# S5's feedthrough table by products on four column tiles, two masked copies and four shifted DMAs, with the first table loads on GpSimd's queue

## Chip, cores and metric

The kernel runs on one core of one Trainium2 chip. The metric is the device time of one execution in microseconds (us), lower is better. The engines are TensorE (PE, with its weight loads as PEld), VectorE (DVE), ScalarE (ACT), GpSimd (POOL) and SyncE (SP), which mostly issues DMAs.

## The reference

A decoder trunk of two layers on x (256 rows of 1024, float32). Each layer is: half a SwiGLU feed-forward block, a token mixer, half a SwiGLU feed-forward block, each behind an RMS norm and added to h. Layer 0 mixes with S5, a diagonal state-space layer; layer 1 with block-sparse attention.

```python
def s5_mixer(h, w_in, a_re, a_im, log_dt, b_re, b_im, c_re, c_im, d_skip, w_glu, w_out):
    u = h @ w_in
    lam = exp((a_re + i a_im) * exp(log_dt))        # 64 groups of 64 states
    # per group of 16 channels: state[t] = lam * state[t-1] + B u[t];  y[t] = Re(C state[t])
    y = y + d_skip * u
    g = gelu(y)
    g = g * sigmoid(g @ w_glu)
    return g @ w_out
```

So y is, for each group of 16 channels, a causal convolution of u with the taps C lam^k B, and d_skip added to the tap at distance 0.

## The kernel before

The trunk runs phase by phase: f00 (feed-forward), s5, f01, f10, moba, f11. Weights stream from HBM through three raw buffers on SP's DMA queue; ACT and DVE split each into a high and a low part in fp32r (L84 and L85, or with a gain L90 and L91), and PE makes three products for one (L397 to L399, L424, L425, L428). `st.pump()` starts such splits; SP's next weight load waits until a raw buffer has been split.

S5 handles four time steps at a time. For each block b of 128 channels (eight of them, as four groups of 32 channels, the index q) it reads three tables from DRAM scratch: dA (from input to state), dE (phases), and dB, of which columns 0 to 1023 lead from state to output and columns 1024 to 1535 are the feedthrough table: per q a matrix of 128 x 128, input step s and channel by output step t and channel, zero where t is before s, else the tap at distance t - s, with d_skip on the tap at distance 0. Within 32 channels there are two groups of 16 that must not mix, so products over 32 channels are masked by group.

The tables depend on weights alone. The generator `tables` makes them while f00 runs: its pieces are put, by a clock in units of matmul work (`slot`), between f00's matmuls, so the order on each engine is fixed in the program. An early part on POOL computes the sines and powers of lam (L691 to L697, behind POOL's part of the first norm, L1363 and following), DVE then makes the phases E (L631) and, block by block, the products `ZC`. `spread(b)` copies them into `TT` and `MPs[b]` with the groups apart (L857, L858) and writes `TT` to dB (L860); `d_diag(b)` puts d_skip on a diagonal. Then `t3_tab(b)` makes the feedthrough table (L878 to L895): eight f32 matmuls of 32 output rows and 64 columns into the first 32 partitions of a PSUM tile, one for each q and each of the real and the imaginary part (L887); one more that adds the diagonal (L889); eight ACT copies with a scale `gm` of 0 or 1 by group (L893), which place the taps for input step s at partitions 32s and at output steps s to 3 of the tile `t3`, whose other places were zeroed once (L647); and one DMA to dB (L895). `t1_tab` transposes and writes dA (L867 to L870).

When all is made, the tables' memory is given up, a pool for the loads takes its place, and the first three blocks' loads TA, TE and TB are issued on SP's queue (L944 to L962). SP takes its instructions in order, so S5's fourth w_in load and the loads of w_glu stand behind them. In S5, `w_in` multiplies (L982 scales by the norm, from POOL's L346 to L308), `t1` uses TA on PE (L991), `rot` uses TE on DVE and POOL (L1011 to L1023), and `y_out` uses TB (L1048 to L1050). The later loads follow on SP as buffers come free.

Near the start, DVE's queue holds the copy of transposed parameters `prm` (L671), the mask gm (L674) and `are` (L631) ahead of the splits of x (`xa`, L1346) that PE waits for; POOL makes `i16` (L676).

Of the kernel before, what the change touches and what calls it, by code (L numbers as in the profile page):

```python
# [10 lines left out]
F32 = mybir.dt.float32  # L11
F32R = mybir.dt.float32r
AF = mybir.ActivationFunctionType
OP = mybir.AluOpType
AX = mybir.AxisListType
# [103 lines left out]
def trunk_kernel(ctx: ExitStack, tc, x, ffn_norm, ffn_w_gate, ffn_w_up, ffn_w_down, mix_norm,  # L119
# [3 lines left out]
    nc = tc.nc  # L123
# [13 lines left out]
    def psR():  # L137
        return pp.tile([128, 512], F32, name="pR", tag="R", bufs=2)
# [4 lines left out]
    mm = nc.tensor.matmul  # L143
# [4 lines left out]
    dA = [dp.tile([128, 1024], F32, name=f"dA_{b}") for b in range(NB)]  # L148
    dE = [dp.tile([128, 4 * EW], F32, name=f"dE_{b}") for b in range(2)]
    dB = [dp.tile([128, 1536], F32, name=f"dB_{b}") for b in range(NB)]  # L150
# [84 lines left out]
    ident = cst[:, 0:128]  # L235
# [30 lines left out]
    if "s5" in phases:  # L266
        rho = cp.tile([128, 32], F32, name="rho")
        tstack, lstack, xstack = ExitStack(), ExitStack(), ExitStack()
        tabp = tstack.enter_context(tc.tile_pool(name="tab", bufs=1))
        scn = tabp.tile([32, 2, 128], F32, name="scn")  # L270
        ldt = tabp.tile([32, 2], F32, name="ldt")
        dnat = tabp.tile([32, 32], F32, name="dnat")
        nc.gpsimd.dma_start(ldt, s5_log_dt[0].rearrange("(q g) -> q g", g=2))
        nc.gpsimd.dma_start(scn[:, 0, :], s5_a_re[0].rearrange("(q g) p -> q (g p)", g=2))
        nc.gpsimd.dma_start(scn[:, 1, :], s5_a_im[0].rearrange("(q g) p -> q (g p)", g=2))
        nc.gpsimd.dma_start(dnat, s5_d[0].rearrange("(q c) -> q c", c=32))
    st = Stream(nc, units, rp, hp)

    gT = cp.tile([128, 48], F32, name="gT")
# [343 lines left out]
    def tables(tp):  # L623

        V, P = nc.vector, nc.gpsimd

        def T(name, *shape):
            return tp.tile([128] + list(shape), F32, name=name)
# [9 lines left out]

        MPs = [T(f"mp{k}", 2, 4, 4, 2, 16) for k in range(2)]
        TT = T("tt", 2, 4, 4, 2, 16)  # L640
        t3s = [T(f"t3{k}", 4, 4, 32) for k in range(2)]
        cf7 = T("cf7", 7, 2)
        for k, n in enumerate(range(15, 1, -2)):
            for i in range(2):
# [21 lines left out]
        ps = psR()  # L666
# [2 lines left out]
        nc.tensor.transpose(ps[:, 64:96], dtb.rearrange("q g p -> q (g p)"), ident[0:32, 0:32])  # L669
        prm = T("prm", 3, 32)  # L670
        V.tensor_copy(prm.rearrange("p a b -> p (a b)"), ps[:, 0:96])  # L671
        gm = tp.tile([32, 2], F32, name="gm")
        i2 = ident[0:32, 0:32].rearrange("p (g n) -> p g n", g=2)
        V.reduce_sum(gm, i2, axis=AX.X)  # L674
        i16 = tp.tile([32, 16], F32, name="i16")
        P.tensor_tensor(i16, i2[:, 0], i2[:, 1], op=OP.add)  # L676
        dTq = T("dTq", 32)
        ar, ai, dt = prm[:, 0, :], prm[:, 1, :], prm[:, 2, :]
        are, aim, mag = T("are", 32), T("aim", 32), T("mag", 32)
        tt(are, ar, dt, OP.mult)  # L680
# [3 lines left out]
        yield  # L684

        ps = psR()
        nc.tensor.transpose(ps[0:32, 0:32], dnat, ident[0:32, 0:32])
        V.tensor_copy(dTq[0:32, :], ps[0:32, 0:32])

        def pt(o, a, b, op):  # L690
            P.tensor_tensor(o, a, b, op=op)  # L691
# [33 lines left out]
        q, y, y2, e0, e1, den = (T(n, 32) for n in ("q", "y", "y2", "e0", "e1", "den"))  # L725
# [125 lines left out]
        def spread(b):  # L851

            d_diag(b)
            tv, mv = (o.rearrange("p i q s g n -> p (i q) s g n") for o in (TT, MPs[b % 2]))
            zv = ZC[b].rearrange("p m i q (s n) -> p m (i q) s n", n=16)
            for g, r in enumerate(HALF):
                nc.scalar.activation(tv[r, :, :, g, :], zv[r, 0, :, 1:5], AF.Copy)  # L857
                nc.scalar.activation(mv[r, :, :, g, :], zv[r, 1, :, 1:5], AF.Copy)  # L858
            for i in range(2):
                nc.gpsimd.dma_start(dB[b][:, 512 * i:512 * i + 512].rearrange("p (q x) -> p q x", q=4),  # L860
                                    TT[:, i].rearrange("p q t g n -> p q (t g n)"))
# [10 lines left out]
        DG = {}  # L872

        def d_diag(b):
            DG[b] = tp.tile([32, 4, 16], F32, name="dg", bufs=2)
            P.tensor_tensor(DG[b], i16[:, None, :].to_broadcast([32, 4, 16]),
                            dTq[0:32, 4 * b:4 * b + 4, None].to_broadcast([32, 4, 16]), op=OP.mult)

        def t3_tab(b):

            t3 = t3s[b % 2]
            ps = psR()
            zc = ZC.pop(b)
            pk = ps[0:32, 0:256].rearrange("p (q t c) -> p q t c", q=4, c=16)
            for qq in range(4):
                for i in range(2):
                    mm(ps[0:32, qq * 64:(qq + 1) * 64], MPs[b % 2][:, i, qq, 3].rearrange("p g n -> p (g n)"),  # L887
                       zc[:, 0, i, qq, 0:64], start=qq == 0 and i == 0, stop=False, skip_group_check=True)
            mm(pk[:, :, 0, :], ident[0:32, 0:32], DG.pop(b), start=False, stop=True, skip_group_check=True)  # L889
            tv = t3.rearrange("p q t (g c) -> p q t g c", c=16)  # L890
            for s in range(4):
                for g in range(2):
                    nc.scalar.activation(tv[32 * s:32 * s + 32, :, s:4, g, :], pk[:, :, 0:4 - s, :], AF.Identity,  # L893
                                         scale=gm[:, g:g + 1])
            nc.gpsimd.dma_start(dB[b][:, 1024:1536], t3.rearrange("p q t c -> p (q t c)"))  # L895

        work = []

# [10 lines left out]
        def add_spread(b):  # L909
            work.append((0.0, B_AT, (spread, b), [(t3_tab, b), (t1_tab, b, 0), (t1_tab, b, 1)], 3 * (b - 1)))  # L910
# [15 lines left out]
        while work or later or dma:  # L926
# [4 lines left out]
            if later and later[0][0] <= now:  # L931
                f = later.pop(0)
                f[1](*f[2:])
                done[0] += 1
            while work and work[0][1] <= now and credit >= work[0][0] and done[0] >= work[0][4]:
                w, _, f, pe, _ = work.pop(0)
                f[0](*f[1:])
                credit -= w
                t = max([now + LAG] + [a[0] + PACE for a in later])
# [2 lines left out]
        tstack.close()  # L942
        LP.append(lstack.enter_context(tc.tile_pool(name="load", bufs=3)))
        for b in range(3):  # L944
            ld_a(b)
            ld_e(b)
        for b in range(3):
            ld_b(b)

    LP, TA, TE, TB = [], {}, {}, {}  # L950

    def ld_a(b):
        TA[b] = LP[0].tile([128, 1024], F32, name="TA", bufs=3)
        nc.sync.dma_start(TA[b], dA[b])

    def ld_e(b):
        TE[b] = LP[0].tile([128, 2, 4, 65], F32, name="TE", bufs=3)
        nc.sync.dma_start(TE[b], dE[b // 4].rearrange("p (i q c) -> p i q c", i=2, c=65)[:, :, (b % 4) * 4:(b % 4) * 4 + 4])

    def ld_b(b):  # L960
        TB[b] = LP[0].tile([128, 1536], F32, name="TB", bufs=3)
        nc.sync.dma_start(TB[b], dB[b])  # L962


    def s5(nxt, entry):
# [60 lines left out]
        def t1ld(b):  # L1026
            t1(b)
            if b + 3 < NB:
                ld_a(b + 3)
# [5 lines left out]
        def rot_ld(b):  # L1035
            rot(b)
            if 0 < b < NB - 2:
                ld_e(b + 2)
# [269 lines left out]

    pre = []
    tab = tables(tabp) if "s5" in phases else iter(())  # L1310
    next(tab, None)
    slot = [0]
# [72 lines left out]
    ps = psR()  # L1385
# [73 lines left out]
```

## Time and profile before

| | |
|---|---|
| median of 3 runs | 992.19 us (992.04 to 992.23) |
| the profiled execution: its time, its span | 992.93 us, 991.2 us |
| granted TensorE clock | 1.000 |
| PE, PEld, DVE, ACT, POOL busy | 980.8, 878.8, 702.9, 575.9, 167.4 us |
| L893, ACT's copies of the feedthrough table | x64, 287 to 468 ns each, 97.0 to 200.4 us |
| DMAs of the feedthrough table (L895) | x8, 256 KB each, median 3.6 us from issue to landing |
| loads TA, TE, TB | x8 each, 512, 260 and 768 KB, median 5.5, 4.6 and 6.3 us to landing |

Times in a row are microseconds from the span's start; the span is from the first to the last instruction of the profiled execution, and a little time lies around it. A row of the timeline gives start, length, engine, line, operation, output<-input by the program's names, shapes and a count; the bracket at its end gives the engine's idle time before it and what ended that. Matmul rows overlap: a row's length is that of one matmul from its first to its last part, and the step from start to start is what it costs. An f32 matmul stands as two records. In a row of `L887 ... 106/110/110`, the three numbers are least, median and greatest length in ns.

### The profile page before, as it was taken

Reading aid. Unit: us, or ns where it says so; the run is one execution under the profiler, and the core shown is the slowest. Engines: PE = TensorE matmul, PEld = TensorE weight load, DVE = VectorE, ACT = ScalarE, POOL = GpSimd, SP = SyncE. Lnnn points to the kernel's source line nnn. Section 1 sums busy time; section 2 is a strip of 40 time slices with the busy share of each in tenths; the row PEclk is TensorE's granted clock in tenths of the full one; section 3 lists DMA queues with packets and bytes.
Section 4 is the critical chain, followed back from the end, with each engine's and each line's share of the span. In section 5 each row is a group of like instructions: output and inputs, shape, how many; then the busy total and the mean of one; then the engine's idle time right before and its main releaser. Section 6 shows DMA issues by size and latency. Waiting matters only on the chain.

```text
span 991.2 us, 16683 instructions
## 1 busy us (share of the span) xinstructions
PE 980.8 (99%) x6448; PEld 878.8 (89%) x6448; DVE 702.9 (71%) x1147; ACT 575.9 (58%) x1045; POOL 167.4 (17%) x330
## 2 busy tenths in 40 slices
PE   9999999999999999999999999999999999999998
PEld 7778888888998999999989999999888899999997
DVE  5699676857978677666657776665689667776663
ACT  6647778754246655555545555553798665655551
POOL 5881222103750100000010000000442010000000
PEclk9999999999999999999999999999999999999999
DMA  8978776887735566555626765655344456666531
GB/s 236 277 262 256 264 256 213 268 300 261 268 126 197 191 209 213 179 205 183 200 86 216 237 226 172 212 171 175 129 165 135 166 169 215 210 217 207 176 129 42
DMA packets 138080, 198.64 MB, mean 200 GB/s; under 512 B 16321, under 2 KB 109585, under 8 KB 137745
## 3 DMA queue, kind: packets, MB, share of 16 engines
q1 hardware_dynamic: 133808, 184.32, 57.0%
q0 software_dynamic: 3616, 12.66, 3.3%
q8 instruction: 50, 0.82, 0.3%
q10 hardware_dynamic: 576, 0.61, 0.3%
q14 instruction: 30, 0.24, 0.1%
HBM read 183.89 MB, written 13.66 MB: 199 GB/s over the span
## 4 chain that ended last, share of the span: by engine, by line
PE 89%; DVE 5%; POOL 3%; issue 1%; ACT 1%; DMA 1%; SPq 0%; ACTq 0%; DVEq 0%
PE pM L557 12%; PE pM L556 12%; PE pM L558 12%; PE pA L428 9%; PE pA L424 9%; PE pA L425 9%; PE pM L397 5%; PE pM L398 5%; PE pM L399 5%; DVE wlo L85 1%; POOL sc L691 1%; PE pR L331 1%; PE pR L887 1%; PE pR L867 1%; DVE zo L1016 1%
## 5 line engine op out<-in xcount | busy, mean ns | idle before, releaser
L556 PE MATMUL pM<-xa,whi 128*128 128x256 f32 x1056 | 293.0, 277 | 0.0
L557 PE MATMUL pM<-xa,whi 128*128 128x256 f32 x1056 | 292.3, 277 | 0.0
L558 PE MATMUL pM<-xa,wlo 128*128 128x256 f32 x1056 | 291.8, 276 | 0.0
L91 DVE SCALAR_TENSOR_TENSOR wlo<-raw,gT,whi 128x512 fp32r<-128x512 f32 x328 | 228.1, 748 | 69.6 <-ACT whi L90 69.3
L85 DVE TENSOR_TENSOR wlo<-raw,whi 128x1024 fp32r<-128x1024 f32 (+1 forms) x157 | 191.7, 1235 | 57.0 <-ACT whi L84 53.1
L90 ACT ACTIVATE whi<-raw,gT 128x512 fp32r<-128x512 f32 x328 | 213.6, 711 | 17.7 <-PE pA L428 13.6
L557 PEld LDWEIGHTS pM<-xa,whi 128*128 128x128 f32 x1056 | 198.5, 188 | 0.3
L556 PEld LDWEIGHTS pM<-xa,whi 128*128 128x128 f32 x1056 | 198.3, 188 | 0.0
L558 PEld LDWEIGHTS pM<-xa,wlo 128*128 128x128 f32 x1056 | 198.3, 188 | 0.0
L84 ACT ACTIVATE whi<-raw 128x1024 fp32r<-128x1024 f32 (+1 forms) x157 | 160.9, 1049 | 27.1 <-DMA raw<-in_ffn_w_down_dram 7.4
L424 PE MATMUL pA<-whi,ah 128*128 128x512 f32 x352 | 138.5, 394 | 0.0
L428 PE MATMUL pA<-whi,al 128*128 128x512 f32 (+1 forms) x409 | 137.8, 360 | 0.0
L425 PE MATMUL pA<-wlo,ah 128*128 128x512 f32 x352 | 137.4, 390 | 0.0
L571 ACT ACTIVATE sg<-gr 128x256 f32<-128x256 f32 x66 | 27.6, 418 | 158.7 <-DVE gr L568 158.7
L397 PE MATMUL pM<-whi,xa 128*128 128x512 f32 x288 | 119.4, 415 | 0.0
L398 PE MATMUL pM<-wlo,xa 128*128 128x512 f32 x288 | 112.9, 392 | 0.2 <-DVE wlo L91 0.2
L399 PE MATMUL pM<-whi,xa 128*128 128x512 f32 x288 | 113.0, 392 | 0.0
L428 PEld LDWEIGHTS pA<-whi,al 128*128 128x128 f32 x409 | 76.8, 188 | 16.4
L346 POOL TENSOR_TENSOR ms<-ss 128x1 f32<-128x1 f32 x10 | 1.9, 194 | 466.8 <-ACT sq L343 466.8
L424 PEld LDWEIGHTS pA<-whi,ah 128*128 128x128 f32 x352 | 66.1, 188 | 11.5
L425 PEld LDWEIGHTS pA<-wlo,ah 128*128 128x128 f32 x352 | 66.1, 188 | 11.3
L568 DVE TENSOR_TENSOR gr<-pM,rrow 128x512 f32<-128x512 f32 x66 | 45.5, 689 | 33.9 <-PE pM L558 33.8
(266 smaller groups left out, 1274.0 us busy)
## 6 DMA issues: line engine op xcount, KB each, us to landing
raw<-in_ffn_w_down_dram SPq DMA_DIRECT2D x44, 1024.0 KB, 5.3
raw<-in_ffn_w_gate_dram SPq DMA_DIRECT2D x80, 512.0 KB, 4.0
raw<-in_ffn_w_up_dram SPq DMA_DIRECT2D x80, 512.0 KB, 5.2
raw<-in_moba_w_qkv_dram SPq DMA_DIRECT2D x12, 1024.0 KB, 5.1
TB<-dB SPq DMA_DIRECT2D x8, 768.0 KB, 6.3
raw<-in_ffn_w_gate_dram SPq DMA_DIRECT2D x16, 256.0 KB, 4.3
raw<-in_ffn_w_up_dram SPq DMA_DIRECT2D x16, 256.0 KB, 4.6
dB<-tt POOLq DMA_DIRECT2D x16, 256.0 KB, 4.4
```

Source lines behind the costliest of these rows:

```text
L85: nc.vector.tensor_tensor(lo[:, c], r[:, c], hi[:, c].bitcast(F32), op=OP.subtract)
L90: nc.scalar.activation(hi[:, c], r[:, c], AF.Identity, scale=g)
L91: nc.vector.scalar_tensor_tensor(lo[:, c], r[:, c], g, hi[:, c].bitcast(F32), op0=OP.mult, op1=OP.subtract)
L397: mm(o, xh, wh, start=start, stop=False)
L398: mm(o, xh, wl, start=False, stop=False)
L399: mm(o, xl, wh, start=False, stop=stop)
L424: mm(o, xh, wh[:, c], start=first and kk == kks[0], stop=False)
L425: mm(o, xh, wl[:, c], start=False, stop=False)
L428: mm(o[:, a:a + w], xl, wh[:, n * 512 + a:n * 512 + a + w], start=False, stop=stop)
L556: mm(o, a, xh, start=k == 0 and i == 0, stop=False, skip_group_check=True)
L557: mm(o, a, xl, start=False, stop=False, skip_group_check=True)
L558: mm(o, b, xh, start=False, stop=k == 7, skip_group_check=True)
```

## The change

The feedthrough table is made in another form. `t3_tab(b)` now writes the four q onto four column tiles of PE (32 output rows each, PSUM partitions 32q to 32q + 31), 64 columns each: 4 products of the real part, 4 of the imaginary part, and 4 that add the diagonal, each with 32 columns of the 128 x 128 identity against `DG`, now 128 x 16. Two ACT copies of all 128 partitions, masked by group, put the four taps into `t3`, now 7 steps x 2 groups x 16 with the first three steps zero. The placing by input step is left to four DMAs of 64 KB each: for s, all partitions read 128 elements that begin at step 3 - s, and go to rows 32s to 32s + 31 of dB.

So d_skip is loaded as 8 x 128 in place of 32 x 32 and transposed to `dT` of 128 x 8; the masks `gm` and `i16` are made for 128 partitions, both by reductions on DVE; `d_diag` is one product with a scalar per partition.

The first loads of TA, TE and TB, three blocks, go to POOL's queue in place of SP's.

On PE, at the first table, there stands before (`zc` are the products, `mp` the spread copies, `dg` the diagonal, `whi`, `wlo` and `xa` f00's operands):

```order
L397 MATMUL pM<-whi,xa 128x512
L398 MATMUL pM<-wlo,xa 128x512
L399 MATMUL pM<-whi,xa 128x512
L887 MATMUL pR<-zc,mp_143 32x64 x8
L889 MATMUL pR<-dg,cst 32x4x16
L397 MATMUL pM<-whi,xa 128x512
L398 MATMUL pM<-wlo,xa 128x512
```

And now:

```order
L397 MATMUL pM<-whi,xa 128x512
L398 MATMUL pM<-wlo,xa 128x512
L399 MATMUL pM<-whi,xa 128x512
L885 MATMUL pR<-zc,mp_143 32x64 x8
L888 MATMUL pR<-dg,cst 32x16 x4
L397 MATMUL pM<-whi,xa 128x512
L398 MATMUL pM<-wlo,xa 128x512
```

The place among f00's matmuls is the same; the one diagonal matmul has become four, and the eight alternate between column tiles.

On DVE, at the start of the program, where PE waits for `xa`, there stands in the difference:

```order
 L85 TENSOR_TENSOR wlo<-raw,whi 128x1024
 L671 COPY prm<-pR 128x96
-L674 TENSOR_REDUCE gm<-cst 32x2
+L673 TENSOR_REDUCE gm<-cst 128x2
+L674 TENSOR_REDUCE i_245<-cst 128x16
 L631 TENSOR_TENSOR are<-prm 128x32
 L1346 SCALAR_TENSOR_TENSOR xa<-pA_253,gT,xa 128x256
```

One reduction has grown and a second has come ahead of `are` and `xa`; on POOL, L676 has gone, so that L1363 follows the memsets.

On POOL, at the end of the table work and ahead of the norm of S5's input, there stands before:

```order
L723 DMA dE_89<-e 128x2080
L870 DMA dA_87<-t_2188 128x512
L870 DMA dA_87<-t_2218 128x512
L346 TENSOR_TENSOR ms<-ss 128x1
L347 TENSOR_SCALAR ms<-ms 128x1
```

And now:

```order
L867 DMA dA_87<-t_2218 128x512
L954 DMA TA<-dA_80 128x1024
L958 DMA TE<-dE_88 128x2x260
L954 DMA TA<-dA_81 128x1024
L958 DMA TE<-dE_88 128x2x260
L954 DMA TA<-dA_82 128x1024
L958 DMA TE<-dE_88 128x2x260
L962 DMA TB<-dB_90 128x1536
L962 DMA TB<-dB_91 128x1536
L962 DMA TB<-dB_92 128x1536
L346 TENSOR_TENSOR ms<-ss 128x1
```

The nine loads have come between the last table's DMA and the norm; on SP they are gone from between the third and the fourth w_in load.

```diff
-        dnat = tabp.tile([32, 32], F32, name="dnat")
+        dnat = tabp.tile([8, 128], F32, name="dnat")
...
-        t3s = [T(f"t3{k}", 4, 4, 32) for k in range(2)]
+        t3s = [T(f"t3{k}", 7, 2, 16) for k in range(2)]
...
-        gm = tp.tile([32, 2], F32, name="gm")
-        i2 = ident[0:32, 0:32].rearrange("p (g n) -> p g n", g=2)
-        V.reduce_sum(gm, i2, axis=AX.X)
-        i16 = tp.tile([32, 16], F32, name="i16")
-        P.tensor_tensor(i16, i2[:, 0], i2[:, 1], op=OP.add)
-        dTq = T("dTq", 32)
+        gm, i16, dT = T("gm", 2), T("i16", 16), T("dT", 8)
+        V.reduce_sum(gm, ident.rearrange("p (q g n) -> p g q n", q=4, g=2), axis=AX.XY)
+        V.reduce_sum(i16, ident.rearrange("p (a n) -> p n a", n=16), axis=AX.X)
...
-        nc.tensor.transpose(ps[0:32, 0:32], dnat, ident[0:32, 0:32])
-        V.tensor_copy(dTq[0:32, :], ps[0:32, 0:32])
+        nc.tensor.transpose(ps[:, 0:8], dnat, ident[0:8, 0:8])
+        V.tensor_copy(dT, ps[:, 0:8])
...
         def d_diag(b):
-            DG[b] = tp.tile([32, 4, 16], F32, name="dg", bufs=2)
-            P.tensor_tensor(DG[b], i16[:, None, :].to_broadcast([32, 4, 16]),
-                            dTq[0:32, 4 * b:4 * b + 4, None].to_broadcast([32, 4, 16]), op=OP.mult)
+            DG[b] = tp.tile([128, 16], F32, name="dg", bufs=2)
+            P.tensor_scalar(DG[b], i16, dT[:, b:b + 1], None, op0=OP.mult)
...
-            pk = ps[0:32, 0:256].rearrange("p (q t c) -> p q t c", q=4, c=16)
-            for qq in range(4):
-                for i in range(2):
-                    mm(ps[0:32, qq * 64:(qq + 1) * 64], MPs[b % 2][:, i, qq, 3].rearrange("p g n -> p (g n)"),
-                       zc[:, 0, i, qq, 0:64], start=qq == 0 and i == 0, stop=False, skip_group_check=True)
-            mm(pk[:, :, 0, :], ident[0:32, 0:32], DG.pop(b), start=False, stop=True, skip_group_check=True)
-            tv = t3.rearrange("p q t (g c) -> p q t g c", c=16)
+            dg = DG.pop(b)
+            for x in range(3):
+                for q in range(4):
+                    r = slice(q * 32, q * 32 + 32)
+                    if x < 2:
+                        mm(ps[r, 0:64], MPs[b % 2][:, x, q, 3].rearrange("p g n -> p (g n)"), zc[:, 0, x, q, 0:64],
+                           start=x == 0, stop=False, skip_group_check=True)
+                    else:
+                        mm(ps[r, 0:16], ident[:, r], dg, start=False, stop=True, skip_group_check=True)
+            for g in range(2):
+                nc.scalar.activation(t3[:, 3:7, g, :], ps[:, 0:64].rearrange("p (t c) -> p t c", c=16), AF.Identity,
+                                     scale=gm[:, g:g + 1])
+            tf = t3.rearrange("p t g c -> p (t g c)")
             for s in range(4):
-                for g in range(2):
-                    nc.scalar.activation(tv[32 * s:32 * s + 32, :, s:4, g, :], pk[:, :, 0:4 - s, :], AF.Identity,
-                                         scale=gm[:, g:g + 1])
-            nc.gpsimd.dma_start(dB[b][:, 1024:1536], t3.rearrange("p q t c -> p (q t c)"))
+                nc.gpsimd.dma_start(dB[b][32 * s:32 * s + 32, 1024:1536].rearrange("p (q x) -> q p x", q=4),
+                                    tf[:, 96 - 32 * s:224 - 32 * s])
...
         for b in range(3):
-            ld_a(b)
-            ld_e(b)
+            ld_a(b, nc.gpsimd)
+            ld_e(b, nc.gpsimd)
         for b in range(3):
-            ld_b(b)
+            ld_b(b, nc.gpsimd)
...
-    def ld_a(b):
+    def ld_a(b, eng=nc.sync):
         TA[b] = LP[0].tile([128, 1024], F32, name="TA", bufs=3)
-        nc.sync.dma_start(TA[b], dA[b])
+        eng.dma_start(TA[b], dA[b])
```

`ld_e` and `ld_b` take `eng` in the same way.

More of the change, by code (lines that the diff above doesn't have):

```diff
@@ L275, in trunk_kernel @@
         nc.gpsimd.dma_start(scn[:, 1, :], s5_a_im[0].rearrange("(q g) p -> q (g p)", g=2))
-        nc.gpsimd.dma_start(dnat, s5_d[0].rearrange("(q c) -> q c", c=32))
+        nc.gpsimd.dma_start(dnat, s5_d[0].rearrange("(b c) -> b c", c=128))
     st = Stream(nc, units, rp, hp)
@@ L944, in tables, with ld_e, ld_b @@
         for b in range(3):
-            ld_a(b)
-            ld_e(b)
+            ld_a(b, nc.gpsimd)
+            ld_e(b, nc.gpsimd)
         for b in range(3):
-            ld_b(b)
+            ld_b(b, nc.gpsimd)
     LP, TA, TE, TB = [], {}, {}, {}
-    def ld_a(b):
+    def ld_a(b, eng=nc.sync):
         TA[b] = LP[0].tile([128, 1024], F32, name="TA", bufs=3)
-        nc.sync.dma_start(TA[b], dA[b])
-    def ld_e(b):
+        eng.dma_start(TA[b], dA[b])
+    def ld_e(b, eng=nc.sync):
         TE[b] = LP[0].tile([128, 2, 4, 65], F32, name="TE", bufs=3)
-        nc.sync.dma_start(TE[b], dE[b // 4].rearrange("p (i q c) -> p i q c", i=2, c=65)[:, :, (b % 4) * 4:(b % 4) * 4 + 4])
-    def ld_b(b):
+        eng.dma_start(TE[b], dE[b // 4].rearrange("p (i q c) -> p i q c", i=2, c=65)[:, :, (b % 4) * 4:(b % 4) * 4 + 4])
+    def ld_b(b, eng=nc.sync):
         TB[b] = LP[0].tile([128, 1536], F32, name="TB", bufs=3)
-        nc.sync.dma_start(TB[b], dB[b])
+        eng.dma_start(TB[b], dB[b])
     def s5(nxt, entry):
```

## Prediction

> **What bounds the kernel now.** I read the page first, then the busy time by stretches, the timeline of the stretch that holds the table work, the chain of waits, and last the timelines of the queues that the change touches. The first line below is the page's busy time by engine, the second its chain of work that ended last.
>
> ```profile
> PE 980.8 (99%) x6448; PEld 878.8 (89%) x6448; DVE 702.9 (71%) x1147; ACT 575.9 (58%) x1045; POOL 167.4 (17%) x330
> ...
> PE 89%; DVE 5%; POOL 3%; issue 1%; ACT 1%; DMA 1%; SPq 0%; ACTq 0%; DVEq 0%
> ```
>
> PE has little idle time to win. The stretches show where the other 11% of the chain lie. Columns: stretch, its length, busy time of PE, of its weight loads, DVE, ACT, POOL, then the clock, DMA share and GB/s.
>
> ```profile
> 45.00:68.00 23.00, 21.17 (x102) 16.64 (x100) 22.34 (x43) 11.03 (x20) 22.13 (x44) 1.00 0.69 209
> 68.00:95.00 27.00, 26.92 (x122) 22.23 (x123) 25.26 (x34) 16.84 (x24) 5.55 (x12) 1.00 0.80 260
> 95.00:210.00 115.00, 115.00 (x643) 93.06 (x642) 80.27 (x116) 86.17 (x164) 27.33 (x51) 1.00 0.75 259
> 210.00:238.00 28.00, 27.89 (x136) 22.87 (x134) 17.19 (x26) 16.32 (x33) 3.82 (x14) 1.00 0.89 313
> 238.00:300.00 62.00, 61.94 (x510) 60.05 (x509) 54.66 (x99) 20.20 (x39) 36.48 (x32) 1.00 0.54 187
> ```
>
> Up to 68 us PE waits now and then for DVE and POOL (23.00 - 21.17 = 1.8 us in 45 to 68). From 68 to 300 it waits for next to nothing, at full clock. All eight feedthrough tables are made between 95 and 210, and S5's own products follow. So two things count: PE's own time for the tables, and anything that comes later before 68. ACT time saved after 95 counts for nothing by itself.
>
> **The change part by part: PE.** The last of the eight blocks, on PE; columns are start, length, line, and operands:
>
> ```profile
> 195.67 0.39 PE L399 MATMUL pM<-whi,xa 128*128 128x512 f32 x1
> ...
> 196.35 0.39 PE L399 MATMUL pM<-whi,xa 128*128 128x512 f32 x1
> 196.67 1.08 PE L887 MATMUL pR<-zc,mp 128*32 128x64 f32 x16
> 197.68 0.29 PE L889 MATMUL pR<-dg,cst 32*32 32x64 f32 x2
> 197.91 0.50 PE L397 MATMUL pM<-whi,xa 128*128 128x512 f32 x1
> 198.24 0.39 PE L398 MATMUL pM<-wlo,xa 128*128 128x512 f32 x1
> ```
>
> Ordinary matmuls start every 0.227 us (195.67 to 196.35 is three steps, with one L397 and one L398 between). From 196.35 to 198.24 are 1.89 us; less two ordinary steps, the block costs 1.44 us, and eight blocks 11.5 us. By pieces: entry 196.67 - 196.35 - 0.23 = 0.09; the products 197.68 - 196.67 = 1.01; the diagonal's two records and the turn out of them 0.23; exit 198.24 - 197.91 - 0.23 = 0.10. Each product in f32 is two records, so 8 are 16. One record's own length is in the next rows.
>
> ```profile
> L887 PEld LDWEIGHTS pR<-zc,mp x128: 106/110/110, 95.7 to 197.5; 128*32 128x32 f32 x128
> L887 PE MATMUL pR<-zc,mp x128: 219/219/243, 95.7 to 197.5; 128*32 128x64 f32 x128
> ```
>
> (1.08 - 0.22) / 15 gives a step of 0.057 us; 16 steps are 0.90, and 0.11 of the 1.01 go to start-up and to the turn to the diagonal's 32-row form. The eight products stay, on the same 128 rows and 64 columns, but now stand on four column tiles in turn. No row of this trace has two column tiles side by side, so I bound the step. Without overlap it stays 16 x 0.057 = 0.90. If each product's first record runs under the previous product's second, a product costs one step: 8 x 0.057 = 0.45. Four tiles wholly side by side would be 0.22. I take 0.53, near the one-step case, since the two records of a product share a tile and must follow each other, while the next product has a tile of its own; the 0.01 a product is for a start that is not instant.
>
> The diagonal: two records become four products, 8 records, of 16 columns on 128 rows. A 16-column record streams a quarter of 64 columns, 0.014 us; a step no shorter than now would be 0.057. So 8 x 0.014 = 0.11 to 8 x 0.057 = 0.45; I take 0.23, some 0.03 each, half a step, since neighbours differ in tile here too. The turn to the 32-row form goes (0.11 less 0.02 of start-up); the turn out of the block, 0.23 less two steps or some 0.10, stays, as does the exit of 0.10. New block: 0.09 + 0.02 + 0.53 + 0.23 + 0.20 = 1.07. Saved: 0.37 each, **3.0 us** in all. At the ends: 0.09 + 0.02 + 0.45 + 0.11 + 0.20 = 0.87 (4.6 us saved) and 0.09 + 0.02 + 0.90 + 0.45 + 0.20 = 1.66 (1.8 lost).
>
> The Trainium skill, TensorEngine Tiling (Array Packing), Overview, gives up to four times the speed for a small dimension of 32 or less. By it the products would be 0.22 and the block 0.09 + 0.02 + 0.22 + 0.23 + 0.20 = 0.76, an estimate by that page that saves 5.4 us in all; nothing in the trace of before shows it.
>
> **ACT and DMA.** ACT's eight masked copies of a block become two, from 32-partition pieces to 128 x 64:
>
> ```profile
> 198.01 2.69 ACT L893 ACTIVATE t<-pR,gm 32x256 f32<-32x256 f32 x8 [2.14 <-PE pR L889]
> ...
> 200.99 0.54 POOL L895 DMA_DIRECT2D dB<-t  x1 [6.18 <-ACT t L893]
> ```
>
> 2.69 us become at most two times a 128 x 256 copy of 0.38 (row of L1070 below), 0.8; some 15 us of ACT in 115, priced at nothing, for PE never waited there. POOL issues four DMAs of 64 KB in place of one: three more at 0.54 are 1.6 us a block, 13 us in all, behind which POOL's copy of the next chunk and ACT-fed table DMAs stand; ACT ends 1.9 us earlier, which pays for it, and POOL is busy 27 of 115 us. Nothing.
>
> **The start.** The masks gm and i16 are now reduced over 128 partitions on DVE, i16 no longer on POOL. The chain there, and the reduction's nearest rows (32 elements; 256 from PSUM):
>
> ```profile
> 12.11 0.08 DVE gm L674
> 12.19 0.14 DVE are L631
> 12.33 0.41 DVE xa L1346
> ...
> 12.78 0.83 PE pA L1338 x4
> ...
> 18.42 0.62 ACT sq L1360 x2
> ...
> 19.10 0.64 POOL ms L1363
> ```
> ```profile
> 12.02 0.16 DVE L674 TENSOR_REDUCE gm<-cst 32x2 f32<-32x32 f32 x1
> ...
> L1225 DVE TENSOR_REDUCE mx<-pA x8: 412/415/417, 737.3 to 772.1; 128x1 f32<-128x256 f32 x8
> ```
>
> (412 - 160) / 224 is 1.1 ns an element; 96 more for gm are 0.11 us, and i16 with 128 takes 0.08 + 0.11 = 0.19. That is 0.30 us ahead of xa, for which PE stands idle, and the chain carries it through ACT to POOL at 19.10. At POOL:
>
> ```profile
> 7.72 0.71 POOL L676 TENSOR_TENSOR i<-cst 32x16 f32<-32x16 f32 x1
> 19.10 0.63 POOL L1363 TENSOR_TENSOR ms<-ss 128x2 f32<-128x2 f32 x1 [10.67 <-ACT sq L1360]
> 19.82 0.19 POOL L1364 TENSOR_SCALAR ms<-ms 128x2 f32<-128x2 f32 x1
> ...
> 45.48 0.22 DVE L706 COPY e<-c 128x16 f32<-128x16 f32 x1 [3.86 <-POOL c L697]
> ```
>
> L676 was POOL's first such operation, in idle time. If its long 0.71 was a first call's price, up to 0.71 - 0.19 = 0.5 moves to L1363; if not, nothing. I take 0.2, as L1363 is itself already long. DVE waits 3.86 us for this POOL run at 45, so it arrives there whole, and DVE is full (22.34 of 23) until 68. The start costs **0.5 us** (0.3 to 0.8). The smaller memsets and the dnat load lie in POOL's idle time before 19.10: nothing.
>
> **The first loads.** SP's and POOL's queues, ACT's use of the norm and of the fourth w_in load, the time to landing of the table writes (in the list of issues) and of TA's loads, and the first use of a table on PE:
>
> ```profile
> 201.52 0.54 POOL L723 DMA_DIRECT2D dE<-e  x1
> 207.81 0.54 POOL L870 DMA_DIRECT2D dA<-t  x1 [3.34 <-ACT t L869]
> 222.87 0.19 POOL L346 TENSOR_TENSOR ms<-ss 128x1 f32<-128x1 f32 x1 [14.52 <-ACT sq L343]
> ...
> dA<-t POOLq DMA_DIRECT2D x16, 256.0 KB, 4.3
> ...
> 211.02 0.35 SPq L954 DMA_DIRECT2D TA<-dA  x1
> ...
> 216.85 0.53 SPq L185 DMA_DIRECT2D raw<-in_s_w_in_dram  x1
> ...
> 230.10 0.69 ACT L982 ACTIVATE us<-pM,rr 128x512 f32<-128x512 f32 x1 [1.25 <-POOL rs_e L307]
> 230.69 2.55 ACT L90 ACTIVATE whi<-raw,gT 128x512 fp32r<-128x512 f32 x4
> ...
> DMA to landing us min/median/max: 3.2/5.5/7.3
> ...
> 237.50 1.75 PE pA L991 x16
> ...
> 278.57 0.38 ACT L1070 ACTIVATE gf<-pR 128x256 f32<-128x256 f32 x1 [4.77 <-DVE xa L1069]
> ```
>
> SP's wait for the table memory held the w_in load until 216.85; now it goes earlier, but ACT split it at 230.69, 14 us after the issue, and did not wait for it (no bracket). Gain: nothing. On POOL the first load waits for the last table DMA (207.81 + 4.3, about 212); nine issues of 0.54 end at 217. By the program the ninth waits until the first has landed: 212 + 7.3 = 219.4, then 0.5. Behind them stands L346 at 222.87 with the norm of S5's input: 3 us to spare, and the first user of the norm is ACT at 230.10. The tables are first used at 237.50.
>
> **Sum.** -3.0 + 0.5 = **-2.5 us**. The profiled execution has a span of 991.2 in a time of 992.93 us; I expect a span of 988.7. The median of the runs shown is 992.19, 0.74 below the profiled one; taking the 2.5 off it gives **989.7**.
>
> **The rivals.** *Serial tiles:* products on different column tiles don't overlap. For it: no row shows an overlap. Then the block is 0.09 + 0.02 + 0.90 + 0.11 to 0.45 + 0.20 = 1.32 to 1.66, so -1.0 to +1.8 us over eight, with the start -0.7 to +2.6: 991.5 to 994.8, 992.5 in the middle of the lower half. *Loads in the open (the other side):* each change of column tile holds the next weight load until the running matmul is done. Twelve changes at the 0.110 us of a load are 1.3 us a block; over serial products 1.32 + 1.3 = 2.6, so 8 x 1.2 + 0.5, +10 us: about 1002. Set against the forecast's block it decides once a change costs over 0.03 us (0.37 / 12). Against it: loads of 110 ns already start every 57 ns under matmuls on the same rows. The Trainium skill, TensorE: Matmul & The Clock Gate, Part 3, says that a weight load overlaps a running matmul only when their row group differs, and all four tiles here span all rows; the rows of L887 speak against it, at least within a tile. *POOL late:* if each of the nine loads took POOL 2 us, they would end at 212 + 18 = 230, L346 7 us late and the norm's first user at 230.10 up to 7 late; part of that PE would wait out, so 0 to 5 us on top of the forecast: 989.7 to 994.7. Every POOL DMA shown takes 0.54.
>
> **How the numbers follow.** Overlap as forecast 0.62, serial 0.24, loads in the open 0.06, POOL late 0.08. A difference of 0.2%, 2 us, is about what a measurement of this kernel can tell. Within the forecast case the time runs from 987.9 (block 0.87, start 0.3) to 991.2 (half-way to serial: block 1.25, start 0.5); three quarters of it are below 990.2. That gives faster 0.47, same 0.40 (0.15 of the forecast case, 0.20 serial, 0.05 POOL late), slower 0.13. The range 987.5 to 993.6 also takes in a little more overlap than the forecast and the lower part of serial tiles; it leaves out the open loads and the far ends, under 2 in 10.
>
> **What would show it.** Starts in the block: from the matmul ahead of L885 to the second one behind L888 1.5 us (1.07 and two steps) instead of 1.89, with rows of different tiles starting under 57 ns apart; the two ACT copies under 0.8 us together; DVE's xa at about 12.6 in place of 12.25 and POOL's L1363 at 19.4; L346 with PE's stream, 2 to 3 us earlier than 222.87. Wrong would be: a block as long as before, a wait of PE between 68 and 300, or an L346 behind a load.

## The result and the profile after

The changed kernel took 986.11 us (median of 4 runs, 985.81 to 987.16), the kernel before 992.21 us beside it (4 runs, 992.04 to 992.8). The ratio is 0.9939 with a 95% interval of 0.9922 to 0.9957: faster by 6.1 us, where 2.5 were forecast, and below the range's lower end of 987.5. The profiled execution took 986.17 us with a span of 984.4; before they were 992.93 and 991.2.

The page's busy time by engine of the changed kernel first, then its busy time in the stretch of the tables (stretch, length, PE, weight loads, DVE, ACT, POOL, clock, DMA share, GB/s):

```profile
PE 974.3 (99%) x6496; PEld 873.9 (89%) x6496; DVE 702.3 (71%) x1148; ACT 559.1 (57%) x997; POOL 193.3 (20%) x362
```
```profile
95.00:210.00 115.00, 115.00 (x721) 93.21 (x720) 83.35 (x122) 72.63 (x121) 51.62 (x84) 1.00 0.83 277
```

PE is as full between 95 and 210 as it was, at the same clock, but has more matmul records there (721 in place of 643). 48 of the 78 more are the diagonal's (24 records a block in place of 18); the other 30 are work that came after 210 us in the kernel before, so the same 115 us now hold more of what follows. ACT lost 13.5 us there (86.17 to 72.63) and POOL gained 24. The last of the eight blocks, in the timeline of PE (start, length, engine, line, operation, operands, count):

```profile
190.29 0.39 PE L399 MATMUL pM<-whi,xa 128*128 128x512 f32 x1
190.61 0.43 PE L885 MATMUL pR<-zc,mp 128*32 128x64 f32 x16
190.86 0.23 PE L888 MATMUL pR<-dg,cst 128*32 128x16 f32 x8
191.02 0.50 PE L397 MATMUL pM<-whi,xa 128*128 128x512 f32 x1
191.35 0.39 PE L398 MATMUL pM<-wlo,xa 128*128 128x512 f32 x1
```

From the L399 ahead to the second matmul behind, 190.29 to 191.35, are 1.06 us where there were 1.89; less two ordinary steps of 0.227 the block costs 0.61 in place of 1.44. The 16 records of the products take 0.43 from the first start to the last end; one record takes 0.22, so the starts lie (0.43 - 0.22) / 15 = 0.014 us apart on average, where they lay 0.057 apart. In the records' own times they come in four groups of four, 7 ns apart within a group, and the groups start at 0, 80, 136 and 191 ns. Before, the records of the one tile started at 0, 80, 136 and 192 ns and so on. So the starts fit four tiles side by side, each at the old step. Over the eight blocks 11.37 us have become 4.75 (one block counts 0.12 less in both kernels, because the row ahead of it, an L500, has a step of 0.11 and not of 0.227). That is 6.6 us: the whole of the gain of 6.1 and half a microsecond more, which the start seems to take back, as told below.

### The profile page after: what moved, and what is told of

Same layout as the page of the kernel before. It is cut to its first block, busy times and chain, and to the rows that moved or that the text cites. A ratio compares the mean times of both kernels' runs of the same rounds, so it can differ in the third digit from the quotient of the medians.

```text
span 984.4 us, 16782 instructions
## 1 busy us (share of the span) xinstructions
PE 974.3 (99%) x6496; PEld 873.9 (89%) x6496; DVE 702.3 (71%) x1148; ACT 559.1 (57%) x997; POOL 193.3 (20%) x362
## 4 chain that ended last, share of the span: by engine, by line
PE 91%; DVE 3%; POOL 3%; ACT 1%; DMA 1%; issue 1%; SPq 0%; ACTq 0%
PE pM L557 12%; PE pM L556 12%; PE pM L558 12%; PE pA L428 9%; PE pA L424 9%; PE pA L425 9%; PE pM L397 6%; PE pM L398 6%; PE pM L399 6%; DVE wlo L85 1%; POOL sc L688 1%; PE pR L331 1%; PE pR L1050 1%; PE pR L1049 1%; PE pR L1048 1%
## 5 line engine op out<-in xcount | busy, mean ns | idle before, releaser
L397 PE MATMUL pM<-whi,xa 128*128 128x512 f32 x288 | 119.3, 414 | 0.0
L399 PE MATMUL pM<-whi,xa 128*128 128x512 f32 x288 | 112.9, 392 | 0.0
```

The lines of the kernel that those rows point to most:

```text
L397: mm(o, xh, wh, start=start, stop=False)
L399: mm(o, xl, wh, start=False, stop=stop)
```

## The experiments

All times stand beside the kernel before on the same chip; its median lay between 992.12 and 992.52 in these. In the expectations, A, B, T and C are names of theories, told there.

**The loads alone.** The kernel before with its nine first loads on POOL's queue:

```diff
-            ld_a(b)
-            ld_e(b)
+            ld_a(b, nc.gpsimd)
+            ld_e(b, nc.gpsimd)
...
-            ld_b(b)
+            ld_b(b, nc.gpsimd)
```

> The kernel before with only the nine first loads moved to POOL's queue. Theory A (the gain is PE's own time, because the column tiles run side by side; nothing else counts): no change, 992.2 within 0.5 us, and PE without a wait between 68 and 300. Theory B (half the gain comes from the loads, since SP's fourth w_in load no longer stands behind them, or from ACT's freed time): 1 to 3 us faster than before, 989 to 991.

Measured: 992.2 us, ratio 0.9998 (0.9989 to 1.0007). The loads' new queue gives nothing and costs nothing.

**The table alone.** The changed kernel with the same lines put back on SP's queue.

> The changed kernel with the first loads back on SP's queue: the table part alone. Theory A: all of the gain, 986.1 within 0.7 us. Theory B: 987 to 989, since the loads' share is missing.

Measured: 986.06 us, ratio 0.9938 (0.9923 to 0.9953). The table part holds all of the gain.

**The order of the tiles, two by two and one by one.** In the first kernel both parts of tiles 0 and 1 come ahead of tiles 2 and 3; in the second each tile's two products stand together:

```diff
-            for x in range(3):
-                for q in range(4):
+            for x, q in [(x, p + q) for p in (0, 2) for x in range(2) for q in range(2)] + [(2, q) for q in range(4)]:
```
```diff
-            for x in range(3):
-                for q in range(4):
+            for x, q in [(x, q) for q in range(4) for x in range(2)] + [(2, q) for q in range(4)]:
```

> The changed kernel with the eight products in another order: tiles 0 and 1, both parts, then tiles 2 and 3, so that only two column tiles are neighbours. Same instructions, same result. Theory A: the products take two lanes, 8 x 0.057 = 0.46 in place of 0.25 us, the block 0.82 in place of 0.61, eight blocks +1.7 us: 987.8. Theory B or a gain from fewer ACT copies: 986.1, unchanged. If tiles had queues of their own, so that order did not matter: block 0.61, 986.1.

> The changed kernel with the products tile by tile (real and imaginary part of tile 0, then of tile 1 and so on), so that two neighbours share a tile except at three places. Theory A, tiles run side by side only as neighbours in order: products 13 to 16 steps of 0.057, 0.74 to 0.91 us, block 1.10 to 1.27, eight blocks +3.9 to +5.3 us: 990.0 to 991.4, most of the gain gone though ACT's copies, the DMAs and the loads are as in the changed kernel. Theory B: 986 to 988. If tiles had queues of their own: block 0.6 to 0.7, 986 to 987.

Measured: 986.69 us, ratio 0.9948 (0.9932 to 0.9965), and 986.36 us, ratio 0.9940 (0.9925 to 0.9955). The forecast's own theory, that only neighbours in the program overlap, missed here, in both kernels: a block costs 0.63 us in both, where it gave 0.82 and at least 1.10. A block of the second, with the products tile by tile:

```profile
122.24 0.39 PE L399 MATMUL pM<-whi,xa 128*128 128x512 f32 x1
122.55 0.45 PE L884 MATMUL pR<-zc,mp 128*32 128x64 f32 x16
122.80 0.25 PE L887 MATMUL pR<-dg,cst 128*32 128x16 f32 x8
122.98 0.50 PE L397 MATMUL pM<-whi,xa 128*128 128x512 f32 x1
123.32 0.40 PE L398 MATMUL pM<-wlo,xa 128*128 128x512 f32 x1
```

The 16 records last 0.45 in place of 0.43 of the changed kernel, and the whole block costs 0.63 in place of 0.61. The starts still come in groups of four, now 13 ns apart within a group. So a tile's four records do not hold back the next tile's.

**More products, spread or on one tile.** Each block makes its eight products a second time, into columns 256 to 319, which nothing reads; in one kernel on the four tiles, in the other all on tile 0:

```diff
+            for x in range(2):
+                for q in range(4):
+                    mm(ps[q * 32:q * 32 + 32, 256:320], MPs[b % 2][:, x, q, 3].rearrange("p g n -> p (g n)"), zc[:, 0, x, q, 0:64],
+                       start=x == 0, stop=x == 1, skip_group_check=True)
```
```diff
+            for q in range(4):
+                for x in range(2):
+                    mm(ps[0:32, 256:320], MPs[b % 2][:, x, q, 3].rearrange("p g n -> p (g n)"), zc[:, 0, x, q, 0:64],
+                       start=x == 0, stop=x == 1, skip_group_check=True)
```

> The changed kernel with each block's eight products made a second time, into columns that nothing reads, spread over the four column tiles as the first eight are. Theory T (the four tiles work side by side and each has its own order of work, so that a block lasts as long as its longest tile): 16 more records in four groups, 0.25 us more a block, 8 x 0.25 = +2.0 us on 986.1, so 988.1. Theory C (the records of the new form are short wherever they write, some 0.25 us for 16; before, they were long for another reason): the same, 988.1. The two part in the next kernel.

> The changed kernel with each block's eight products made a second time, into columns that nothing reads, all on column tile 0. As many instructions of the same size as in the kernel with the spread copies. Theory T: 16 records on one tile at a step of 0.057 us are 0.90 us a block, 8 x 0.90 = +7.2 us on 986.1, so 993.3. Theory C: 0.25 us a block, +2.0 us, 988.1.

Measured: 987.73 us, ratio 0.9956 (0.9939 to 0.9972), and 993.21 us, ratio 1.0011 (1.0001 to 1.0020). A block of the first, then of the second; L891 is the copy:

```profile
122.65 0.43 PE L885 MATMUL pR<-zc,mp 128*32 128x64 f32 x16
122.90 0.23 PE L888 MATMUL pR<-dg,cst 128*32 128x16 f32 x8
122.96 0.41 PE L891 MATMUL pR<-zc,mp 128*32 128x64 f32 x16
123.30 0.50 PE L397 MATMUL pM<-whi,xa 128*128 128x512 f32 x1
```
```profile
125.04 0.43 PE L885 MATMUL pR<-zc,mp 128*32 128x64 f32 x16
125.29 0.23 PE L888 MATMUL pR<-dg,cst 128*32 128x16 f32 x8
125.35 1.06 PE L891 MATMUL pR<-zc,mp 128*32 128x64 f32 x16
126.34 0.50 PE L397 MATMUL pM<-whi,xa 128*128 128x512 f32 x1
```

The same 16 records take 0.41 us on four tiles and 1.06 on one, with steps of (0.41 - 0.22) / 15 = 0.013 and (1.06 - 0.22) / 15 = 0.056. Over eight blocks they add 1.95 and 7.1 us on PE, and 1.6 and 7.1 us to the time. Theory C is out: the records are not short by their form, but by standing side by side. And what PE does in a block goes into the time nearly one to one.

**The products back on one tile.** Only the diagonal's matmuls stay on four tiles. The two sums are kept apart and the copies read the diagonal's part alone, so the table lacks the products:

```diff
-                        mm(ps[r, 0:64], MPs[b % 2][:, x, q, 3].rearrange("p g n -> p (g n)"), zc[:, 0, x, q, 0:64],
-                           start=x == 0, stop=False, skip_group_check=True)
+                        mm(ps[0:32, q * 64:q * 64 + 64], MPs[b % 2][:, x, q, 3].rearrange("p g n -> p (g n)"), zc[:, 0, x, q, 0:64],
+                           start=x == 0, stop=x == 1, skip_group_check=True)
...
-                        mm(ps[r, 0:16], ident[:, r], dg, start=False, stop=True, skip_group_check=True)
+                        mm(ps[r, 256:272], ident[:, r], dg, start=True, stop=True, skip_group_check=True)
```

> The changed kernel with the products back on column tile 0, side by side in four ranges of columns as before, and only the diagonal's on four tiles (the sums of the two are not formed, and the copies read the diagonal's part alone). Theory T: the 16 product records take 0.90 in place of 0.25 us, a block 0.61 + 0.65 = 1.26, 8 x 0.65 = 5.2 us back, 991.3; what then is left of the gain, 0.9 to 1.4 us, is the diagonal's. Rival: the gain lies mostly in the diagonal and the turns, then 989 or less.

Measured: 991.57 us, ratio 0.9997 (0.9987 to 1.0006). The block costs 1.26, as worked out; 5.2 of the 6.6 us are the products'. The other 1.4 come from the diagonal: its four products stand on the form that PE is in already, and on four tiles, in place of two records on another form. Before, its first record started 0.149 us behind the last product's, where a step is 0.056. No run separates the form from the four tiles here. The block also shows who passes whom (L885 are all ahead of L888 in the program):

```profile
123.40 1.02 PE L885 MATMUL pR<-zc,mp 128*32 128x64 f32 x15
124.22 0.22 PE L888 MATMUL pR<-dg,cst 128*32 128x16 f32 x3
124.27 0.22 PE L885 MATMUL pR<-zc,mp 128*32 128x64 f32 x1
124.27 0.27 PE L888 MATMUL pR<-dg,cst 128*32 128x16 f32 x5
```

Three of the diagonal's records start ahead of the last product's, but only then: for 0.8 us three tiles stood empty while their work was behind tile 0's in the program. At 124.22 three records waited for tile 0, the last product's and two of the diagonal's. With one every 3.3 ns (7 ns for a product's two, 13 ns for a tile's four) this fits a rule: records are handed out in the order of the program, and a tile takes four, one running and three waiting; a fifth holds up all that is behind it. The rule is an inference from the starts. The next kernel was made to test that.

**Eight records a tile, tile by tile.** The products twice, as above, but all of a tile's ahead of the next tile's:

```diff
+            for q in range(4):
+                r = slice(q * 32, q * 32 + 32)
+                for c in (256, 0):
+                    for x in range(2):
+                        mm(ps[r, c:c + 64], MPs[b % 2][:, x, q, 3].rearrange("p g n -> p (g n)"), zc[:, 0, x, q, 0:64],
+                           start=x == 0, stop=c > 0 and x == 1, skip_group_check=True)
```

> The changed kernel with the eight products of a block made twice as in the kernel with the spread copies, but in the order of the tiles: all four products of tile 0 (8 records), then tile 1's, and so on, and the diagonal last. In the runs so far the starts fit this: records are handed out in program order, one every 3.3 ns, and a tile takes four of them, one running and three waiting. Theory T with that limit: tile 1 gets its first record when tile 0's eighth is taken, some 4 x 0.056 = 0.22 us after the start, tile 2 another 0.22 later; the products last 3 x 0.22 + 8 x 0.056 = 1.12 in place of 0.25, a block 0.61 + 0.87 = 1.48, 8 x 0.87 = +7.0 us on 986.1, 993.1. Theory T without a limit (any order will do): 0.25 us more a block as with the spread copies, 987.7 to 988.1.

Measured: 993.81 us, ratio 1.0014 (1.0005 to 1.0024). A block in the timeline of PE:

```profile
124.12 0.39 PE L399 MATMUL pM<-whi,xa 128*128 128x512 f32 x1
124.44 1.23 PE L885 MATMUL pR<-zc,mp 128*32 128x64 f32 x29
125.45 0.22 PE L889 MATMUL pR<-dg,cst 128*32 128x16 f32 x3
125.50 0.22 PE L885 MATMUL pR<-zc,mp 128*32 128x64 f32 x1
125.50 0.20 PE L889 MATMUL pR<-dg,cst 128*32 128x16 f32 x3
125.56 0.28 PE L885 MATMUL pR<-zc,mp 128*32 128x64 f32 x2
125.67 0.21 PE L889 MATMUL pR<-dg,cst 128*32 128x16 f32 x2
125.81 0.50 PE L397 MATMUL pM<-whi,xa 128*128 128x512 f32 x1
126.15 0.39 PE L398 MATMUL pM<-wlo,xa 128*128 128x512 f32 x1
```

The block costs 126.15 - 124.12 - 0.45 = 1.57 us where the same 32 product records in the other order cost 0.85, so the order alone gave up 5.8 us over the eight. The 1.57 are 0.09 more than the 1.48 worked out, for a tile's first step is 80 ns and not 56, and the way to the next tile takes 6 ns, three times over. By the records' own starts, one tile works alone for the first 0.25 us (0, 80, 136, 191 and 247 ns); the next tile's first start comes at 253, just behind the fifth, when by the rule the eighth has found a place. A limit of five would let it start behind the fourth record, at about 0.2 us, and a limit of three behind the sixth, at about 0.31. Worked out record by record (a step of 56 ns for 64 columns and 28.5 for 16, 24 more for a tile's first record, one record handed out every 3.35 ns), the rule with four gives every start of one block of each of the five orders within 9 ns; with three or five, starts of this kernel are off by over 200 ns. The trace doesn't name a record's tile, so the rule remains a fit to the starts.

**ACT's relief undone.** The changed kernel with six more copies in each block:

```diff
+            junk = tp.tile([128, 64], F32, name="junk", bufs=2)
+            for _ in range(6):
+                nc.scalar.activation(junk, ps[:, 0:64], AF.Identity, scale=gm[:, 0:1])
```

> The changed kernel with six more copies of 128 x 64 on ACT in each block, into a tile that nothing reads: ACT gets back most of the 2.2 us a block that the change took from it (6 x 0.32 = 1.9). My theory: PE never waited for ACT in 95 to 210, so 986.1 within 0.6, and the block on PE still 0.61. Rival: part of the gain is ACT's relief, at least 0.2 us a block, so 987.7 or more.

Measured: 986.23 us, ratio 0.9939 (0.9924 to 0.9954); a block still costs 0.61. The row of the added copies:

```profile
L891 ACT ACTIVATE junk<-pR,gm x48: 292/314/318, 96.5 to 192.8; 128x64 f32<-128x64 f32 x48
```

48 copies of 0.314 us put 15 us back on ACT, and the time did not move.

**The masks later.** The changed kernel with its two reductions moved from the start to just ahead of the first table piece:

```diff
-        V.reduce_sum(gm, ident.rearrange("p (q g n) -> p g q n", q=4, g=2), axis=AX.XY)
-        V.reduce_sum(i16, ident.rearrange("p (a n) -> p n a", n=16), axis=AX.X)
...
+        V.reduce_sum(gm, ident.rearrange("p (q g n) -> p g q n", q=4, g=2), axis=AX.XY)
+        V.reduce_sum(i16, ident.rearrange("p (a n) -> p n a", n=16), axis=AX.X)
         add_e(0)
```

> The changed kernel with the two mask reductions moved from the chain at the start to just ahead of the first table piece. Theory A (the forecast's start term): DVE's xa goes back from 12.63 to about 12.25, POOL's L1363 from 19.50 to about 19.1, and the time is 0.3 to 0.5 lower, 985.6 to 985.8. Rival: the delay is taken up before 68 by other waits, then xa moves as said and the first block on PE stays where it was within the scatter seen there (94.8 to 95.5), 986.1.

Measured: 985.32 us (984.86 to 985.61), ratio 0.9930 (0.9915 to 0.9945). The start of the changed kernel, then of this one:

```profile
11.90 0.25 DVE L671 COPY prm<-pR 128x96 f32<-128x96 f32 x1
...
12.07 0.28 DVE L673 TENSOR_REDUCE gm<-cst 128x2 f32<-128x128 f32 x1
12.26 0.35 DVE L674 TENSOR_REDUCE i<-cst 128x16 f32<-128x128 f32 x1
...
12.53 0.18 DVE L631 TENSOR_TENSOR are<-prm 128x32 f32<-128x32 f32 x1
12.63 0.87 DVE L1346 SCALAR_TENSOR_TENSOR xa<-pA,gT,xa 128x256 fp32r<-128x256 f32 x2
...
19.50 0.61 POOL L1363 TENSOR_TENSOR ms<-ss 128x2 f32<-128x2 f32 x1 [12.24 <-ACT sq L1360]
```
```profile
11.67 0.25 DVE L671 COPY prm<-pR 128x96 f32<-128x96 f32 x1
...
11.95 0.19 DVE L631 TENSOR_TENSOR are<-prm 128x32 f32<-128x32 f32 x1
12.06 0.87 DVE L1346 SCALAR_TENSOR_TENSOR xa<-pA,gT,xa 128x256 fp32r<-128x256 f32 x2
...
18.95 0.62 POOL L1363 TENSOR_TENSOR ms<-ss 128x2 f32<-128x2 f32 x1 [11.69 <-ACT sq L1360]
```

From the copy of `prm` to xa are 0.73 us with the reductions and 0.39 without, as before; to POOL's L1363 are 7.60 and 7.28 (before: 19.10 - 11.86 = 7.24). So the delay of 0.34 is there and reaches POOL whole. The median is 0.8 us under the changed kernel's, more than that; the intervals of the two ratios overlap, so the size is not settled here.

**Blocks joined, and both.** The products stand at once ahead of the first four transposes of the same chunk (L864); in the second kernel the masks are later as well:

```diff
+        def t31_tab(b):
+            t3_tab(b)
+            t1_tab(b, 0)
...
-            work.append((0.0, B_AT, (spread, b), [(t3_tab, b), (t1_tab, b, 0), (t1_tab, b, 1)], 3 * (b - 1)))
+            work.append((0.0, B_AT, (spread, b), [(t31_tab, b), (t1_tab, b, 1)], 2 * (b - 1)))
```

> The changed kernel with each block's products followed at once by the first four transposes of the same chunk's table, also f32, in place of standing alone some 4 to 5 us ahead of them. Theory: what is left of a block's 0.61 us is a third turns between PE's two kinds of matmul, 0.09 in and 0.11 out, and one such pair goes in each of eight places: 8 x 0.2 = 1.6 us, 984.5. Rival: the turns are paid for the transposes' other tile form as well, or the four transposes then wait for the PSUM buffer, and nothing is won: 986.1 or more.

> The same, with the two mask reductions moved from the start to just ahead of the first table piece as well. Theory (0.3 us or more of the start chain reach the end, as the kernel with the masks moved alone showed 0.8): 0.3 to 0.8 below the kernel with the joined blocks alone, about 983.9. Rival (that 0.8 was scatter of the start): within 0.2 of it.

Measured: 985.71 us, ratio 0.9936 (0.9924 to 0.9949), and 985.38 us, ratio 0.9931 (0.9919 to 0.9944). Joining did not bring 1.6 us. A joined block:

```profile
104.73 0.39 PE L399 MATMUL pM<-whi,xa 128*128 128x512 f32 x1
105.05 0.43 PE L885 MATMUL pR<-zc,mp 128*32 128x64 f32 x16
105.30 0.23 PE L888 MATMUL pR<-dg,cst 128*32 128x16 f32 x8
105.46 0.66 PE L864 MATMUL pR<-cst,mp 128*128 128x128 f32 x4
105.87 0.49 PE L397 MATMUL pM<-whi,xa 128*128 128x512 f32 x1
106.20 0.40 PE L398 MATMUL pM<-wlo,xa 128*128 128x512 f32 x1
```

The turn out of the narrow tiles is paid ahead of the transposes, f32 like the products, as it was ahead of L397: 0.16 from L888's first start to the next row in both (105.30 to 105.46, 190.86 to 191.02). So it goes with the tile form, 128*32 to 128*128, and not with the type. Apart, block and transposes cost 0.607 + 0.447 = 1.054 us; joined they cost 1.010, which is 0.35 us over eight and agrees with the 0.4 between the medians. The masks later gave 0.3 more here, about the 0.34 of the start; no difference among the changed kernel, the masks later, the joined blocks and both is outside the intervals. All four beat the kernel before.

## Why the prediction was wrong, step by step

**What bounds the kernel: right.** PE is full from 95 to 210, and what is taken from its blocks comes off the time (extra products on one tile: 7.1 us on PE, 7.1 in the time). ACT's time counted for nothing: put back, it left the time at 986.23, and with ACT relieved as in the changed kernel, the products on one tile took the time back to 991.57, against 992.12 of the kernel before beside it.

**The products' step: wrong, and most of the miss.** The failed step is "I take 0.53, near the one-step case, since the two records of a product share a tile and must follow each other, while the next product has a tile of its own". Two records of one tile do follow each other at 0.057, but more than one neighbour runs beside them: all four tiles do. From the first product's start to the diagonal's are 0.25 us, where the forecast had 0.53 + 0.02 = 0.55: 0.30 a block, 2.4 us. The overlap does not even need different tiles as neighbours in the program: tile by tile, a block costs only 0.02 us more. The value for four tiles side by side stood in the text ("Four tiles wholly side by side would be 0.22") and was left out of the block's ends, which used 0.45; with it the cheap end would have been 0.09 + 0.02 + 0.22 + 0.11 + 0.20 = 0.64, against 0.61 measured. So the range failed by an end that was worked out and then not used. The Trainium skill, TensorEngine Tiling (Array Packing), Overview, gives up to four times the speed at a dimension of 32: the trace agrees, with 0.90 us of steps become 0.22 (0.25 less the start-up), and the sum that went by it, 5.4 us, came nearest.

**The diagonal: wrong by the same step.** 0.23 was taken for 8 records, "half a step, since neighbours differ in tile here too". Their starts span 0.05 us, two records of one tile 29 ns apart and four tiles side by side: 0.18 a block, 1.4 us. Entry (0.09) and turn and exit (0.11 + 0.11 = 0.22 against 0.20) were right within 0.02 us, and the turn to the 32-row form went as said. With 2.4 for the products, and the 0.02 of the exit taken off (0.2 over eight), this is the gap between 3.0 and 6.6.

**The start: the size right, partly by luck.** DVE's 0.30 measured 0.34 and goes to L1363. The first call's price on POOL, 0.2 in the forecast, is not there: L1363 takes 0.61 us as POOL's first operation that is no memset and no DMA, and took 0.63 as the second. Whether 0.34 reaches the end can't be read from before and after alone: POOL's run from L1363 to the c that DVE waits for took 45.23 - 19.10 = 26.13 us before and 45.10 - 19.50 = 25.60 after, and took 25.2 to 26.1 in all these runs. So the first block came at 95.70 before and at 95.51 after. Moving the masks away gave 0.8 and 0.3 us, the sign of the forecast. All kernels together say more. In the ten kernels with the reductions at the start, the time fell 0.15 to 0.95 us short of what PE's blocks had saved, 0.5 on average (6.1 against 6.6 in the changed kernel). In the three without them (the loads alone, the masks later, both) it lay between 0.1 short and 0.3 beyond. That speaks for a start that reaches the end at about the forecast's 0.5, though single kernels scatter too much to show it; the rows account for 0.34, and the rest stays open. The rows of c and of the first block, of before (the block's is 95.70, in the forecast's row of L887) and then of after:

```profile
45.23 0.22 POOL L697 TENSOR_SCALAR c<-e 128x32 f32<-128x32 f32 x1
```
```profile
45.10 0.22 POOL L694 TENSOR_SCALAR c<-e 128x32 f32<-128x32 f32 x1
95.51 0.43 PE L885 MATMUL pR<-zc,mp 128*32 128x64 f32 x16
```

**The loads, ACT and DMAs: rightly priced at nothing, by a working that was off.** A DMA of the table took POOL 0.70 us to issue, not 0.54, so the four of a block cost 2.3 us more than the one before, not 1.6; with the nine loads (5.5 us) that is the 24 us that POOL gained, and PE had no wait between 95 and 210 for it (115.00 of 115.00 us busy). And POOL's first load does not wait until 212 for the last table write: it is issued at 204.85. POOL's timeline of the changed kernel:

```profile
204.85 0.55 POOL L954 DMA_DIRECT2D TA<-dA  x1 [3.38 <-PE pM L399]
...
208.64 1.70 POOL L962 DMA_DIRECT2D TB<-dB  x3
215.94 0.19 POOL L346 TENSOR_TENSOR ms<-ss 128x1 f32<-128x1 f32 x1 [5.59 <-ACT sq L343]
```

The nine issues end at 210.34, not 217, and POOL is idle for 5.59 us ahead of the norm, which ends the rival of POOL late: the loads alone gave a ratio of 0.9998. The loads did land later from there: in the kernel with the loads alone the first three TB came 11.9 to 14.1 us after their issue, and 8.5 to 10.7 before, in both ahead of the first use of a table.

**The rivals.** Serial tiles had 0.24 and loads in the open 0.06; both are out. Weight loads of 0.110 us on the same 128 rows start four at a time, 7 ns apart, and the block has no hole for them. The row of the loads in the changed kernel:

```profile
L885 PEld LDWEIGHTS pR<-zc,mp x128: 106/110/110, 95.5 to 190.8; 128*32 128x32 f32 x128
```

The sentence of the Trainium skill, TensorE: Matmul & The Clock Gate, Part 3, that lets a load overlap a matmul only where the row group differs, does not hold for column tiles here. Nor does its sentence that matmuls start strictly in the order of the program: in the kernel with the products on one tile, three L888 start at 124.22, ahead of an L885 at 124.27 that stands before them.

**The sum.** Blocks 11.37 - 4.75 = 6.6 us less; with the first block 0.2 earlier this is the 6.8 us by which the spans differ (991.2 to 984.4). From the first block to the end of the span were 991.2 - 95.70 = 895.5 us and are 984.4 - 95.51 = 888.9, again 6.6 less, so what stands behind the blocks takes as long as before. The medians differ by 6.1, which is the 6.6 less some 0.5 for the start; the profiled execution of before lay 0.7 over its median.

## What to carry to other kernels

Where an f32 product has 32 output rows, put neighbours on the four column tiles: on a PE that is full, 16 records cost 0.25 us in place of 0.90 and all of it comes off the time. Write them so that no tile has more than about four records (two f32 products) standing ahead of another tile's first: tile by tile was as good with four each (0.63 us a block against 0.61) and lost most of the overlap with eight (1.57 against 0.85). And when an end of an unknown cost has been worked out, the range must contain it, however little the nearest rows speak for it.

## What the runs showed of the hardware

- Column tiles run in their own time, with their own weight loads on the same 128 rows; within one tile an f32 record has a step of 56 ns at 64 columns and of 29 ns at 16; across four tiles the 64-column records start 14 ns apart on average.
- The starts fit a rule by which a record is handed to its tile every 3.3 ns in program order and a tile takes four; then all behind wait (fitted to the starts of five orders within 9 ns, not read from a count in the trace).
- A change between tile forms 128*128 and 128*32 costs 0.09 us on the way in and 0.22 on the way out: 0.11 from the last narrow record to the next row, and 0.11 more in that row's step (0.335 in place of 0.227). The type makes no difference on the way in (0.318 - 0.227 behind the fp32r L399, 0.201 - 0.108 behind the f32 L500), nor to the wait ahead of the next row on the way out. Four f32 transposes of the 128*128 form between fp32r matmuls cost 0.447, four steps of 0.109, so next to nothing for the type.
- The reductions on DVE have 0.28 and 0.35 us in their rows and delay what is behind by 0.34 together, as the rows overlap.
